# First layer's conditioning columns as float32 products in four column groups of the tensor engine, second layer's partial sums inside the first feed-forward

## The chip, the cores and the metric

The kernel is one program on one core of a Trainium2 chip. Its time is the device time of one execution in microseconds (us). The engines are named as in the profile: PE (TensorE matmuls), PEld (the weight loads that belong to them), DVE (VectorE), ACT (ScalarE), POOL (GpSimd) and SP (SyncE, which issues every DMA here).

## The reference

Two layers of a backbone block run over 512 latent tokens and 256 context tokens of width 1024. In each layer a conditioning vector gives six modulation rows per feature, one set for the latent tokens (from `c`) and one for the context tokens (from `c_ctx`):

```python
for layer in range(DEPTH):
    need_ctx = layer < DEPTH - 1
    mod = jax.nn.silu(c) @ w_ada[layer] + b_ada[layer]
    mod_c = jax.nn.silu(c_ctx) @ w_ada[layer] + b_ada[layer]
    sh1, sc1, gt1, sh2, sc2, gt2 = jnp.split(mod[:, None, :], 6, axis=-1)
    ...
    h = rmsnorm(x, g_norm1[layer]) * (1 + sc1) + sh1
    hc = rmsnorm(xc, g_norm1[layer]) * (1 + sc1c) + sh1c
    p = jnp.split(h @ w_in[layer], SPLIT_POINTS, axis=-1)
    ...
    x = x + gt1 * (jnp.concatenate([ya, yb, ym, yd], axis=-1) @ w_out[layer])
    h2 = rmsnorm(x, g_norm2[layer]) * (1 + sc2) + sh2
    x = x + gt2 * sq_relu_ffn(h2, w_ff1[layer], w_ff2[layer])
```

`w_ada[layer]` is 1024 x 6144 float32. The context tokens take the same path in the first layer; in the second, only their first norm is needed (`need_ctx` is false), so the last two thirds of that layer's columns are wanted for one vector only. The four mixers are A (windowed attention), B (dense attention), C (a chunked mLSTM) and D (a chunked state-space scan with a short convolution).

## The kernel before

Activations lie feature-major: 8 chunks of 128 features on the partitions, tokens along the free dimension (256 context, then 512 latent). Every float32 weight tile comes from HBM by an SP DMA (`wraw`, 256 KB, 4 buffers), ACT copies it to float32r (`wh`, line 176) and DVE subtracts the copy from the original (`wl`, line 177). A large product is then three float32r products, h by wh, hl by wh and h by wl, into one PSUM tile. PSUM has three kinds of tiles with two buffers each: `bulk` for the large products, `mx` and `s2` for the mixers.

The order on PE is written by the program. In each layer the mixers run A, D, C, B; each has long chains of small steps over DVE, ACT and POOL, and between these steps `fill` (class `Stream`, lines 368 to 400) emits as many of the next mixer's large products as a credit allows (tables `FILL_*`, lines 38 to 41). Then come the output projection and the feed-forward, `ffn1` (line 1302) and `ffn2` (line 1354), eight blocks each, with PE fed by large products throughout.

The conditioning columns are cut in 24 blocks of 256 columns per layer (`cb`), 1024 x 256 float32 or 1 MB each, with the 1024 rows as 8 blocks `k` of 128. `sil` holds the two vectors after SiLU, 128 x 8 x 2. Three ways of computing a block exist:

- `ada_first` (line 204), for the 8 blocks that the first norm of the first layer needs, before anything else can start. Half a block is one DMA of 512 KB (`adaw`). `ADA_FIRST` gives each half block a letter: P and V split the weights in two float32r parts as above, with the subtraction on POOL or DVE (line 229), and multiply with four columns of `silr`; D multiplies float32 weights directly with `sil2`. The stationary operand has 4 columns in all cases. The 4 x 256 result is copied by ACT (`adarow`), turned by two small products with a constant (`K_CV`), and DVE adds the bias into `mods`.
- `ada_step` (line 257) and `ada_finish` (line 246), for the other 16 blocks of the first layer and 24 of the second. A step issues 8 DMAs of 128 KB (`adar`, 2 buffers, line 270); ACT multiplies each by one entry of `sil` per partition (`adap`, 2 buffers, line 273) and POOL adds it to `acc` (line 275), per vector. This is emitted at a low priority, so that it stands behind other work of the same place. At a later step the sum over partitions is taken by PE, with `acc` stationary and a column of ones (line 252), and DVE adds the bias. For the 16 blocks of the second layer with a single vector, `acc` is first cut into three bfloat16 parts.
- Steps are called at fixed places: three in attention A (lines 697, 698 and 704), four, three and three in the streams of D, C and B (`astep`), one after attention B (line 1249), and 26 in the first layer's feed-forward (lines 1305 and 1306, 1372 and 1373). So 14 of the first layer's 16 jobs lie in its mixers, and the other 2 with all 24 of the second layer in its feed-forward.

The chain that the first norm needs is `norm_scale` (DVE, columns of 128 x 2: `sc`, `rw`, `ry`, `rc`, lines 108 to 116) and then per chunk one ACT operation, one on DVE and the subtraction `hl` on DVE or POOL (line 501).

Of the kernel before, what the change touches and what calls it, by code (L numbers as in the profile page):

```python
# [7 lines left out]
F32 = mybir.dt.float32  # L8
# [22 lines left out]
K_ID, K_LE, K_GE, K_HI, K_CV = 0, 128, 256, 384, 386  # L31
NCST = 388
# [3 lines left out]
ADA_FIRST = "PDPDPDPDPDPVDVPV"  # L36
# bulk products emitted at the steps of the mixers, by layer
# [8 lines left out]
def tile_hybrid_backbone(ctx, tc, xin, cin, wada, win0, win, wout, wf1, wf2, pcol, prow, cst, rope, out):  # L46
# [74 lines left out]
    # constants  # L121
# [23 lines left out]
    # conditioning vectors  # L145
    sil = sm((P, 8, 2), "sil")
# [4 lines left out]
    silr = sm((P, 8, 4), "silr", F32R)  # L151
    V.tensor_copy(silr[:, :, 0:2], sil)
    tt(silr[:, :, 2:4], sil, silr[:, :, 0:2].bitcast(F32), ALU.subtract)
    sil2 = sm((P, 8, 4), "sil2")
    V.memset(sil2, 0.0)
    V.tensor_copy(sil2[:, :, 0:2], sil)
# [4 lines left out]
    # weights: exact split of each float32 weight in two float32r parts; a list over the contraction's blocks  # L161
# [19 lines left out]
    # reciprocal square root of src * scale + eps on small columns  # L181
# [18 lines left out]
    # inputs, and the first norm's shift and scale on the tensor engine  # L200
    xr = [k6(r, (P, 2, NT), name="x") for r in XIN_ROLES]
    raw_roles = [0, 1, 2, 4, 5, 6, 7, 8]

    def ada_first(i, cb):
        pt_ = s2()
        o, oc = pt_[0:4, 0, 0:256], pt_[:, 1, 0:4].rearrange("p (m v) -> p m v", v=2)
        for kh in range(2):
            mode = ADA_FIRST[(2 * i + kh) % len(ADA_FIRST)]
            if i == 7:
# [3 lines left out]
                rk = [raws[k // 2][:, k % 2, :] for k in range(4)]  # L213
            else:
                raw = k6(raw_roles[(2 * i + kh) % 8], (P, 4, 256), name="adaw")
                SY.dma_start(raw, wada[0, cb, kh])
                raws = [raw]
                rk = [raw[:, k, :] for k in range(4)]
            if mode == "D":
                for k in range(4):  # L220
                    mm(o, sil2[:, 4 * kh + k, :], rk[k], kh == 0 and k == 0, kh == 1 and k == 3)
                continue
            E_ = G if mode == "P" else V
            for k in range(0, 4, 2):
                h = T((P, 2, 256), F32R, "wh", 6)
                lo = T((P, 2, 256), F32R, "wl", 6)
                w = raws[k // 2] if i == 7 else raws[0][:, k:k + 2]
                act(h, w, AF.Copy)
                E_.tensor_tensor(lo, w, h.bitcast(F32), ALU.subtract)
                for q in range(2):  # L230
                    mm(o, silr[:, 4 * kh + k + q, :], h[:, q, :], kh == 0 and k + q == 0, False)
                    mm(o, silr[:, 4 * kh + k + q, :], lo[:, q, :], False, kh == 1 and k + q == 3)
        row = tf((4, 256), name="adarow")
        act(row, o, AF.Copy)
        for m in range(2):
            mm(oc[:, m, :], row[:, m * P:(m + 1) * P], cs[0:4, K_CV:K_CV + 2])
        tt(mods[0][:, :, 2 * cb:2 * cb + 2], oc.rearrange("p m v -> p v m"),
           pcs[0][:, C_BADA + 2 * cb:C_BADA + 2 * cb + 2].unsqueeze(1).to_broadcast([P, 2, 2]), ALU.add)
# [3 lines left out]
    ada_jobs = [(0, cb, (0, 1)) for cb in range(8, 24)]  # L242
    ada_jobs += [(1, cb, (0, 1) if cb < 8 else (0,)) for cb in range(24)]
    ada_state = {"i": 0, "pend": []}

# [11 lines left out]
    def ada_step(keep=1, gate=None):  # L257
        i = ada_state["i"]
        ada_finish(keep if i < 24 else 0)
        if i >= len(ada_jobs):  # L260
            return
# [205 lines left out]
    for l in range(DEPTH):  # L467
# [827 lines left out]
        if l == 0:  # L1295
            ada_finish()
# [204 lines left out]
```

## Time and profile before

| | |
|---|---|
| times of three runs | 1895.83, 1904.86 and 1896.25 us, median 1896.25 |
| the profiled execution | span 1897.0 us |
| instructions | 31253 |
| PE busy | 1788.0 us, 94% |
| DVE busy | 1259.2 us, 66% |
| ACT busy | 991.7 us, 52% |
| POOL busy | 553.2 us, 29% |
| HBM read | 172.52 MB, 93 GB/s over the span with the writes |

The profile is of one execution, and its own time is the span, 0.75 us above the median of the three runs. Busy time is instruction time; PE and PEld overlap. The stages can be told apart in the trace by the lines that run in them: 0 to 63 us the first norm and the first conditioning blocks, 63 to 590 the first layer's mixers and output projection, 590 to 1140 its feed-forward, 1140 to 1530 the second layer's mixers, and 1530 to 1897 its feed-forward with the last norm. PEclk is the clock that the throttle granted to TensorE, as a share of full speed.

### The profile page before, as it was taken

To read this page: it belongs to the slowest core of one execution; us is meant where nothing else is said; L and a number is where in the kernel's file an instruction comes from. 1 tells how busy PE (TensorE), PEld (TensorE's weight loads), DVE (VectorE), ACT (ScalarE), POOL (GpSimd) and SP (SyncE) were. 2 spreads that over 40 slices of the span, in tenths; PEclk is the share of its full clock that TensorE was granted. 3 is DMA by queue.
4 is the path that set the end of the run, shared out by engine and by line. 5 is a ranking of instruction groups with operands and counts; after the bars stand their busy time and mean duration, and the time that the engine had idled before them with its cause. 6 is when DMAs were issued, how large, how long until landed. Compare 5 with 4: busy or idle time off the path is not lost.

```text
span 1897.0 us, 31253 instructions
## 1 busy us (share of the span) xinstructions
PE 1788.0 (94%) x11226; PEld 1566.4 (83%) x11226; DVE 1259.2 (66%) x2812; ACT 991.7 (52%) x2082; POOL 553.2 (29%) x655
## 2 busy tenths in 40 slices
PE   5989988998999999999999999999999899999998
PEld 2778887887878888888888887989877699999997
DVE  6668788478887545545645557788588765555556
ACT  4577764656666656544544536553365543333333
POOL 3354466463024655443323412005120100000000
PEclk9999999988999999999999999999999999999999
DMA  6232243223112333333333431123222023222221
GB/s 242 94 91 92 67 128 114 81 76 125 37 48 94 117 110 121 101 121 117 110 100 104 136 114 45 53 64 95 78 78 73 23 85 100 96 95 90 97 92 67
DMA packets 121146, 178.87 MB, mean 94 GB/s; under 512 B 13344, under 2 KB 62880, under 8 KB 120992
## 3 DMA queue, kind: packets, MB, share of 16 engines
q1 hardware_dynamic: 120992, 176.89, 29.3%
q8 instruction: 88, 1.44, 0.3%
q14 instruction: 66, 0.54, 0.1%
HBM read 172.52 MB, written 4.33 MB: 93 GB/s over the span
## 4 chain that ended last, share of the span: by engine, by line
PE 75%; DVE 11%; ACT 6%; POOL 3%; issue 3%; DMA 2%; SPq 0%; DVEq 0%; ACTq 0%; POOLq 0%
PE bulk L97 37%; PE s L97 28%; PE mx L97 8%; POOL acc L275 2%; PE mx L640 2%; DVE wl L108 1%; ACT qs L105 1%; ACT adap L105 1%; DMA adar<-in_wada_dram 1%; ACT wh L105 1%; DMA x<-in_xin_dram 1%; DVE rw L108 1%; ACT pr L105 0%; DVE x L116 0%; DVE xw L108 0%
## 5 line engine op out<-in xcount | busy, mean ns | idle before, releaser
L275 POOL TENSOR_TENSOR acc<-acc,adap 128x256 f32<-128x256 f32 x448 | 369.0, 842 | 393.0 <-ACT adap L105 205.1
L108 DVE TENSOR_TENSOR wl<-wraw,wh 128x512 fp32r<-128x512 f32 (+2 forms) x400 | 292.2, 735 | 117.1 <-ACT wh L105 106.7
L105 ACT ACTIVATE wh<-wraw 128x512 fp32r<-128x512 f32 (+2 forms) x404 | 243.6, 610 | 207.6 <-PE bulk L97 131.6
L105 ACT ACTIVATE adap<-adar,sil 128x256 f32<-128x256 f32 x448 | 218.0, 505 | 187.5 <-DMA adar<-in_wada_dram 127.7
L97 PE MATMUL s<-h,wh 128*128 128x258 f32 (+2 forms) x1024 | 310.6, 313 | 0.0
L97 PE MATMUL s<-hl,wh 128*128 128x258 f32 (+2 forms) x1024 | 301.0, 312 | 0.3 <-DVE hl L116 0.3
L97 PE MATMUL s<-h,wl 128*128 128x258 f32 (+2 forms) x1024 | 246.9, 312 | 0.0
L116 DVE SCALAR_TENSOR_TENSOR x<-bulk,mod,x 128x512 f32<-128x512 f32 (+1 forms) x224 | 149.5, 671 | 114.5 <-PE bulk L97 113.9
L97 PE MATMUL bulk<-ah,wh 128*128 128x512 f32 (+1 forms) x576 | 217.6, 378 | 1.4 <-DVE mod L108 0.8
L97 PE MATMUL bulk<-ah,wl 128*128 128x512 f32 (+1 forms) x576 | 215.8, 375 | 0.0
L97 PE MATMUL bulk<-al,wh 128*128 128x512 f32 (+1 forms) x576 | 215.5, 374 | 0.0
L97 PEld LDWEIGHTS s<-h,wh 128*128 128x128 f32 x1024 | 194.7, 190 | 20.9
L97 PEld LDWEIGHTS s<-hl,wh 128*128 128x128 f32 x1024 | 194.8, 190 | 12.2 <-DVE hl L116 0.7
L97 PE MATMUL bulk<-h,wh 128*128 128x512 f32 (+1 forms) x448 | 166.8, 372 | 5.1 <-DVE ra L108 3.3
L97 PEld LDWEIGHTS s<-h,wl 128*128 128x128 f32 x1024 | 163.6, 190 | 1.1
L97 PE MATMUL bulk<-hl,wh 128*128 128x512 f32 (+1 forms) x448 | 157.9, 352 | 0.0
L97 PE MATMUL bulk<-h,wl 128*128 128x512 f32 (+1 forms) x448 | 157.8, 352 | 0.0
L97 PEld LDWEIGHTS bulk<-ah,wh 128*128 128x128 f32 x576 | 108.2, 188 | 21.5 <-issue 1.2
L97 PEld LDWEIGHTS bulk<-ah,wl 128*128 128x128 f32 x576 | 108.2, 188 | 21.2
L97 PEld LDWEIGHTS bulk<-al,wh 128*128 128x128 f32 x576 | 108.2, 188 | 19.5
L105 ACT ACTIVATE relu<-relu,bs 128x512 f32<-128x512 f32 x96 | 59.0, 644 | 115.2 <-DVE relu L108 114.5
L97 PE MATMUL bulk<-wh,h 128*128 128x256 f32 (+1 forms) x368 | 113.7, 310 | 2.7 <-ACT h L105 1.6
(331 smaller groups left out, 3848.8 us busy)
## 6 DMA issues: line engine op xcount, KB each, us to landing
wraw<-in_wf_dram SPq DMA_DIRECT2D x256, 256.0 KB, 2.8
adar<-in_wada_dram SPq DMA_DIRECT2D x320, 128.0 KB, 2.4
wraw<-in_win_dram SPq DMA_DIRECT2D x80, 256.0 KB, 2.9
wraw<-in_wout_dram SPq DMA_DIRECT2D x32, 256.0 KB, 2.9
adaw<-in_wada_dram SPq DMA_DIRECT2D x14, 512.0 KB, 10.4
x<-in_xin_dram SPq DMA_DIRECT2D x8, 768.0 KB, 6.4
CB<-drows SPq DMA_DIRECT2D x10, 512.0 KB, 6.0
MB<-drows SPq DMA_DIRECT2D x10, 512.0 KB, 5.1
```

The source lines that it names most:

```text
L97: return TE.matmul(o, lhsT=l, rhs=r, start=start, stop=stop)
L105: return S.activation(o, i, f, scale=scale, **kw)
L108: return V.tensor_tensor(o, a, b, op)
L116: return V.scalar_tensor_tensor(o, a, s, b, op0, op1)
L275: G.tensor_tensor(accs[vi], accs[vi], dst, ALU.add)
L640: TE.transpose(tp[:, i, e, :], Ps[e][:, (i0 + i) * P:(i0 + i + 1) * P], ident)
```

## The change

There are three parts.

1. **The first 8 blocks.** `ada_first` no longer splits weights. `sil` lies in the first 16 columns of a tile `silw` of 48 columns, the rest zero. Row block k is a float32 product with the 32 columns of `silw` from 2k on as stationary operand; its result goes to partitions 32 x (k mod 4) on, so that the blocks k = 0 to 3 use four column groups of the array, and k = 4 to 7 add onto them. ACT copies the 128 x 256 result, PE turns it with two transposes, and one DVE reduction adds the four groups up.
2. **The first layer's other 16 blocks** use the same products (`ada0_step`): four DMAs of 256 KB (`ada`, 3 buffers) at a low priority, 8 products into a `bulk` tile, an ACT copy (`adrow`), and at the next step two transposes into another `bulk` tile, the reduction and the bias. ACT's scaling, POOL's sums and the product with ones are gone from them. All 16 now lie in the mixers: three in attention A, six in D's stream, three in C's, three in B's, one after attention B. In the streams each counts 2.0 of credit, and the totals from which the credit is worked out are raised to match (`t_ada`).
3. **The second layer's 24 blocks** keep ACT and POOL and all lie in the first layer's feed-forward. Their DMAs are 256 KB, in tiles of `ta` (5 buffers); ACT's scaling is still 256 wide, POOL's sums are 512 wide over pairs of row blocks, with one more sum of 256 at the end.

```diff
+    silw = sm((P, 48), "silw")
+    V.memset(silw, 0.0)
+    sil = silw[:, 0:16].rearrange("p (k v) -> p k v", v=2)
...
+    def ada_rows(o, kr):
+        for k, w in kr:
+            g = slice(32 * (k % 4), 32 * (k % 4) + 32)
+            mm(o[g, :], silw[:, 2 * k:2 * k + 32], w, k < 4, k >= 4)
+
+    def ada_cols(l, cb, row, oc):
+        for m in range(2):
+            TE.transpose(oc[:, m * P:(m + 1) * P], row[:, m * P:(m + 1) * P], ident)
+        r = sm((P, 2, 2), "adr", bufs=2)
+        V.tensor_reduce(r, oc.rearrange("p (m g i v) -> p v m g i", m=2, g=4, v=2)[:, :, :, :, 0], AX.X, ALU.add)
+        tt(mods[l][:, :, 2 * cb:2 * cb + 2], r,
...
-            if mode == "D":
-                for k in range(4):
-                    mm(o, sil2[:, 4 * kh + k, :], rk[k], kh == 0 and k == 0, kh == 1 and k == 3)
-                continue
-            E_ = G if mode == "P" else V
-            for k in range(0, 4, 2):
...
-                act(h, w, AF.Copy)
-                E_.tensor_tensor(lo, w, h.bitcast(F32), ALU.subtract)
...
+                ada_rows(o, [(4 * kh + k, raw[:, k, :]) for k in range(4)])
+        row = tf((P, 256), name="adarow")
         act(row, o, AF.Copy)
...
+        ada_cols(0, cb, row, oc)
...
+    def ada0_step(gate=None):
+        ada0_finish()
+        cb = ada0["i"]
...
+            raws = [T((P, 2, 256), F32, "ada", 3) for _ in range(4)]
+            for q in range(4):
+                SY.dma_start(raws[q], wada[0, cb, q // 2][:, 2 * (q % 2):2 * (q % 2) + 2, :])
+        o = bulk((P, 256))
+        ada_rows(o, [(k, raws[k // 2][:, k % 2, :]) for k in range(8)])
+        row = T((P, 256), F32, "adrow", 2)
+        act(row, o, AF.Copy)
+        ada0["pend"] = (cb, row)
...
+        with tc.high_priority(offset=-1000000):
+            acc = k4((P, nv, 2, 256), name="acc")
+            for q in range(4):
+                w = ta((P, 2, 256), name="adar")
+                SY.dma_start(w, wada[1, cb, q // 2][:, 2 * (q % 2):2 * (q % 2) + 2, :])
+                for v in range(nv):
+                    dst = acc[:, v] if q == 0 else ta((P, 2, 256), name="adap")
+                    for r in range(2):
+                        act(dst[:, r, :], w[:, r, :], AF.Copy, scale=sil[:, 2 * q + r, v:v + 1])
+                    if q > 0:
+                        G.tensor_tensor(acc[:, v], acc[:, v], dst, ALU.add)
+            for v in range(nv):
+                G.tensor_tensor(acc[:, v, 0, :], acc[:, v, 0, :], acc[:, v, 1, :], ALU.add)
...
-        astep = g_do(ada_step)
+        astep = [g_do(ada0_step, 2.0)] if l == 0 else []
+        t_ada = 2.0 * len(astep)
...
-            gs = gs[:len(od) // 2] + [gstep] + gs[len(od) // 2:] + [gstep]
-            grs.append((lambda g=g: granule(g), gs + [astep]))
+            gs = gs[:len(od) // 2] + [gstep] + (astep if i < 2 else []) + gs[len(od) // 2:] + [gstep]
+            grs.append((lambda g=g: granule(g), gs + astep))
...
-                if cb or b < 2:
-                    ada_step(0 if b == 1 and cb else 1)
+                if l == 0 and (cb or b < 2):
+                    ada_step()
```

On PE in attention A of the first layer, before the change, one job shows only as products of its sums with ones, between the attention's products with the values (`pth`, `ptl` by `VS`) and the transposes of its probabilities (`pr`).

```order
L97 MATMUL mx_1629<-ptl_1635,VS_592 128x256
L97 MATMUL bulk_1741<-ones_67,acc_955 128x1 x2
L97 MATMUL bulk_1741<-ones_67,acc_956 128x1 x2
L97 MATMUL mx_1629<-pth_1689,VS_592 128x256
L640 MATMUL mx_1709<-cst_63,pr_1504 128x128
L640 MATMUL mx_1709<-cst_63,pr_1520 128x128
```

On PE in the same attention after the change, a job is its eight products from the four tiles `ada_1494` to `ada_1497`; the two transposes of the job ahead of it stand four rows above this piece.

```order
L95 MATMUL bulk_1502<-ada_1494,silw_86 32x256 x2
L95 MATMUL bulk_1502<-ada_1495,silw_86 32x256 x2
L95 MATMUL bulk_1502<-ada_1496,silw_86 32x256 x2
L658 MATMUL mx_1513<-cst_63,pr_1301 128x128
L95 MATMUL mx_1421<-pth_1428,VS_483 128x256
L95 MATMUL mx_1421<-ptl_1427,VS_483 128x256
...
L95 MATMUL bulk_1546<-h_100,wh_1069 128x512
L95 MATMUL bulk_1546<-hl_101,wh_1069 128x512
L95 MATMUL bulk_1502<-ada_1497,silw_86 32x256 x2
```

The products of the first three tiles stand together, and those of the fourth come eight rows later: six of attention A, and two of a large product.

On SP, the queue of all DMAs, the same tiles after the change, with the weight loads (`wraw`) that stand among them:

```order
L250 DMA ada_1496<-in_wada_dram 128x512
L168 DMA wraw_1536<-in_win_dram 128x512
L168 DMA wraw_1542<-in_win_dram 128x512
L168 DMA wraw_1923<-in_win_dram 128x512
L168 DMA wraw_1929<-in_win_dram 128x512
L250 DMA ada_1497<-in_wada_dram 128x512
L250 DMA ada_1698<-in_wada_dram 128x512
```

The fourth tile of a job takes the buffer of its first, so its DMA can only be issued when the job's first two products are done.

On POOL in mixer D of the first layer, before the change, the masks of the scan (`CB`) stand among the sums of the conditioning jobs.

```order
L275 TENSOR_TENSOR acc_2627<-acc_2627,adap_2683 128x256
L275 TENSOR_TENSOR acc_2628<-acc_2628,adap_2686 128x256
L938 AFFINE_SELECT CB_3552<-CB_3552 128x512
L939 AFFINE_SELECT CB_3552<-CB_3552 128x512
L938 AFFINE_SELECT CB_3599<-CB_3599 128x512
L939 AFFINE_SELECT CB_3599<-CB_3599 128x512
```

On POOL in mixer D after the change:

```order
L924 MEMSET hst_2998 128x256
L958 AFFINE_SELECT CB_3158<-CB_3158 128x512
L959 AFFINE_SELECT CB_3158<-CB_3158 128x512
L958 AFFINE_SELECT CB_3225<-CB_3225 128x512
L959 AFFINE_SELECT CB_3225<-CB_3225 128x512
```

No conditioning sum is left on POOL ahead of the first feed-forward.

More of the change, by code (lines that the diff above doesn't have):

```diff
@@ L212, in ada_first @@
                     SY.dma_start(raws[q], wada[0, cb, kh][:, 2 * q:2 * q + 2, :])
[L213 removed]
+                ada_rows(o, [(4 * kh + k, raws[k // 2][:, k % 2, :]) for k in range(4)])
             else:
@@ L233, in ada_first @@
-        row = tf((4, 256), name="adarow")
-        act(row, o, AF.Copy)
[L235 to L244, printed above, removed]
@@ L246, in ada_finish @@
-    def ada_finish(keep=0):
-        while len(ada_state["pend"]) > keep:
-            l, cb, vs, accs = ada_state["pend"].pop(0)
-            ap_ = bulk((P, 2, 2))
-            for vi, v in enumerate(vs):
-                for m in range(2):
-                    for t, part in enumerate(accs[vi]):
-                        mm(ap_[:, vi, m:m + 1], part[:, m * P:(m + 1) * P], ones if len(accs[vi]) == 1 else onesb, t == 0, t == len(accs[vi]) - 1)
-            for vi, v in enumerate(vs):
-                tt(mods[l][:, v, 2 * cb:2 * cb + 2], ap_[:, vi, :], pcs[l][:, C_BADA + 2 * cb:C_BADA + 2 * cb + 2], ALU.add)
@@ L257, in ada_step, with ada0_finish @@
[L257 to L260, printed above, removed]
+                ada_rows(o, [(4 * kh + k, raw[:, k, :]) for k in range(4)])
+        row = tf((P, 256), name="adarow")
+        act(row, o, AF.Copy)
+        ada_cols(0, cb, row, oc)
+    ada0 = {"i": 8, "pend": None}
+    def ada0_finish():
+        if ada0["pend"] is not None:
+            cb, row = ada0["pend"]
+            ada_cols(0, cb, row, bulk((P, 256)))
+            ada0["pend"] = None
@@ L266, in ada_step @@
                 st.enter_context(tc.issue_after(gate))
-            accs = [sm((P, 256), "acc", bufs=4) for _ in vs]
-            for k in range(8):
-                w = T((P, 256), F32, "adar", 2)
-                SY.dma_start(w, wada[l, cb, k // 4][:, k % 4, :])
-                for vi, v in enumerate(vs):
-                    dst = accs[vi] if k == 0 else T((P, 256), F32, "adap", 2)
-                    act(dst, w, AF.Copy, scale=sil[:, k, v:v + 1])
-                    if k > 0:
-                        G.tensor_tensor(accs[vi], accs[vi], dst, ALU.add)
@@ new lines, in ada_finish @@
+    def ada_finish():
+        if ada_state["pend"] is None:
+            return
+        cb, parts = ada_state["pend"]
+        ada_state["pend"] = None
+        nv = len(parts)
+        ap_ = bulk((P, 2, 2))
+        for v in range(nv):
+            for m in range(2):
+                for t, part in enumerate(parts[v]):
+                    mm(ap_[:, v, m:m + 1], part[:, m * P:(m + 1) * P], ones if nv == 2 else onesb, t == 0, t == len(parts[v]) - 1)
+        for v in range(nv):
+            tt(mods[1][:, v, 2 * cb:2 * cb + 2], ap_[:, v, :], pcs[1][:, C_BADA + 2 * cb:C_BADA + 2 * cb + 2], ALU.add)
@@ L1390, in tile_hybrid_backbone @@
         ffn2(7, prev)
-        while l == 0 and ada_state["i"] < len(ada_jobs):
+        while l == 0 and ada_state["i"] < 24:
             ada_step()
```

93 lines of the change are left out of this document (43 added, 50 removed).

## Prediction

> **What bounds the kernel now.** I read the page's chain of work first, then busy time by stage, then the chain of waits inside each stage. The span, and the chain's shares by engine:
>
> ```profile
> span 1897.0 us, 31253 instructions
> PE 75%; DVE 11%; ACT 6%; POOL 3%; issue 3%; DMA 2%; SPq 0%; DVEq 0%; ACTq 0%; POOLq 0%
> ```
>
> PE holds three quarters of the chain. The busy time by stage (start:end, length, then busy time of each engine, the granted clock, DMA share):
>
> ```profile
> core 0: us, PE busy (x) PEld busy (x) DVE busy (x) ACT busy (x) POOL busy (x), PEclk, DMA share, GB/s
> 0.00:63.00 63.00, 36.80 (x180) 18.91 (x180) 44.32 (x100) 30.54 (x61) 25.38 (x27) 0.95 0.58 210
> 63.00:590.00 527.00, 485.42 (x3133) 428.34 (x3134) 405.02 (x1010) 339.16 (x775) 225.62 (x273) 0.94 0.28 85
> 590.00:1140.00 550.00, 544.07 (x3182) 475.92 (x3180) 299.12 (x543) 285.06 (x582) 225.35 (x277) 0.99 0.36 114
> 1140.00:1530.00 390.00, 364.07 (x2391) 316.27 (x2392) 304.17 (x793) 206.66 (x451) 76.86 (x79) 0.97 0.21 63
> ```
>
> The first stage (first norm) has PE busy for 37 of 63 us: DVE is ahead of it. The first layer's mixers have PE busy for 92.1% at a clock of 0.94; the second layer's, without conditioning jobs, 93.4% at 0.97. The first feed-forward is full, 544 of 550. The chains of waits by line, for the first layer's mixers, the first stage and the first feed-forward:
>
> ```profile
> by line: PE bulk L97 27.6%; PE s L97 8.2%; POOL acc L275 6.5%; issue 5.7%; PE mx L97 5.3%; PE mx L640 2.9%; ACT adap L105 2.8%; ACT qs L105 2.2%; DMA adar<-in_wada_dram 2.1%; DVE wl L108 2.0%; ACT pr L105 1.5%; DVE xw L108 1.4%; DVE CB L108
> by line: PE s L97 22.1%; DMA x<-in_xin_dram 16.7%; PE mx L97 8.4%; DVE wl L229 8.4%; issue 8.1%; DVE sq L328 6.0%; DVE x L113 5.3%; DVE rc L116 3.9%; DVE sc L116 2.7%; DVE rw L116 2.6%; DVE rw L108 2.6%; SPq L483 2.1%; DVE hl L501 1.8%; SPq
> by line: PE s L97 46.0%; PE bulk L97 36.5%; PE mx L97 15.0%; POOL acc L275 0.8%; DMA adar<-in_wada_dram 0.5%; issue 0.2%; DVE x L116 0.2%; ACT adap L105 0.2%; ACT wh L105 0.2%; DVE xn L116 0.1%; ACT xn L105 0.1%; DVE wl L108 0.1%; DVE sq L3
> ```
>
> In the mixers the conditioning job's own line runs through POOL `acc`, ACT `adap` and DMA `adar`: 6.5 + 2.8 + 2.1 = 11.4% of 527, or 60 us. In the feed-forward it is 0.8 + 0.5 + 0.2 = 1.5% of 550, 8 us. So the change attacks the mixers and the first stage.
>
> **First stage.** Its POOL and DVE subtractions, then three DVE operations on two columns each:
>
> ```profile
> L229 POOL TENSOR_TENSOR wl<-adaw,wh 128x512 fp32r<-128x512 f32 x12 | 16.0, 1352 | 27.4 <-ACT wh L105 27.4
> L229 DVE TENSOR_TENSOR wl<-adaw,wh 128x512 fp32r<-128x512 f32 x4 | 3.1, 797 | 0.0
> L229 DVE TENSOR_TENSOR wl<-wraw,wh 128x512 fp32r<-128x512 f32 x2 | 2.4, 1197 | 0.0
> 35.02 2.53 POOL L229 TENSOR_TENSOR wl<-adaw,wh 128x512 fp32r<-128x512 f32 x2 [1.27 <-ACT wh L105]
> 36.25 1.31 DVE L116 SCALAR_TENSOR_TENSOR sc<-mod,pcol 128x2 f32<-128x2 f32 x2
> 37.67 0.16 DVE L116 SCALAR_TENSOR_TENSOR ry<-rw,ry 128x2 f32<-128x2 f32 x1
> ```
>
> Two columns take DVE 0.16 us, but two such operations took 1.31 us while POOL subtracted. The six subtractions on DVE go, and the chain gives them 8.4% of 63 us = 5.3 us. The held columns `rc`, `sc` and `rw` have 3.9 + 2.7 + 2.6 + 2.6 = 11.8% = 7.4 us; most of that, which I put at 5.7, goes with POOL's 16 us. Added are 8 reductions of a few columns, 8 x 0.16 = 1.3 us at most, mostly in waits for `adaw`. I take -11 us, from -5 (DVE's own subtractions alone) to -13 (all of both). PE, with 26 us idle, hides its 16 transposes.
>
> **First layer's mixers, what goes.** The groups of the job in this stage, and for scale the transposes of A and B:
>
> ```profile
> L275 POOL TENSOR_TENSOR acc<-acc,adap 128x256 f32<-128x256 f32 x203 | 165.7, 840 | 237.9 <-ACT acc L105 130.5 <-ACT adap L105 104.0 <-PE mx L640 2.8
> L105 ACT ACTIVATE adap<-adar,sil 128x256 f32<-128x256 f32 x203 | 97.9, 505 | 62.1 <-POOL acc L275 31.1 <-DMA adar<-in_wada_dram 25.4 <-POOL MB L1166 4.8
> L97 PE MATMUL bulk<-ones,acc 128*128 128x1 f32 x112 | 15.6, 259 | 1.2 <-POOL acc L275 1.2
> L640 PE MATMUL mx<-cst,pr 128*128 128x128 f32 x200 | 33.2, 283 | 5.8 <-ACT pr L105 4.1 <-DVE ptl L108 1.2 <-DVE yB L108 0.3
> ```
>
> POOL loses 166 us, ACT about 100, PE 15.6 us of products with ones (14 jobs). ACT waits 31 us for POOL inside the job, and whatever of the mixers is queued behind such a wait on ACT is late with it. DVE gains too, since its operations last longer beside POOL's: the same operation in the first layer's mixers and in the second's,
>
> ```profile
> L108 DVE TENSOR_TENSOR es<-prow,m 128x1 f32<-128x1 f32 x24 | 7.5, 311 | 0.0
> L108 DVE TENSOR_TENSOR es<-prow,m 128x1 f32<-128x1 f32 x16 | 2.4, 152 | 0.0
> ```
>
> The upper end of this relief is the chain's 60 us. The lower end is PE's busy time at the second layer's share: 485.4 / 0.934 = 520, 7 us less. With that stage's clock as well it is 485.4 x 0.94 / 0.97 / 0.934 = 504, 23 us less. I take -34, the middle of 7 and 60: a chain's 60 us is not all won, because other chains lie just under it, but the job's work is gone from three engines and not from one.
>
> **First layer's mixers, what PE gains in work.** The float32 products of the first stage, a pair of 64-column groups (`vw`) among large products, DVE's eviction of a large product, and the landing time of DMAs of 256 KB and, when the queue is crowded, of 512 KB:
>
> ```profile
> 32.12 1.89 PE L97 MATMUL s<-adaw,sil 128*4 128x256 f32 x8
> L97 PEld LDWEIGHTS s<-adaw,sil 128*4 128x4 f32 x48 | 3.9, 95 | 8.1 <-issue 4.5 <-DVE mod L108 0.8
> 349.85 0.28 PE L97 MATMUL bulk<-wl,h 128*128 128x256 f32 x1
> 349.97 0.28 PE L97 MATMUL bulk<-wh,hl 128*128 128x256 f32 x1
> 350.18 0.45 PE L97 MATMUL mx<-vw,ktok 128*64 128x65 f32 x8
> 350.56 0.39 PE L97 MATMUL bulk<-wh,h 128*128 128x256 f32 x1
> L116 DVE SCALAR_TENSOR_TENSOR x<-bulk,mod,x 128x512 f32<-128x512 f32 (+1 forms) x224 | 149.5, 671 | 114.5 <-PE bulk L97 113.9
> wraw<-in_win_dram SPq DMA_DIRECT2D x80, 256.0 KB, 2.9
> adaw<-in_wada_dram SPq DMA_DIRECT2D x14, 512.0 KB, 10.4
> ```
>
> The 8 records in 1.89 us are 4 products: two records each, one after another, about 0.213 us apiece (the last one's tail taken off). A job has 8 products, 16 records: 16 x 0.213 = 3.41 us if column groups take turns. The row of `vw` says that they do not: 8 records of 65 columns in two groups take 0.45 us with one tail of about 0.22, 33 ns a record, where 0.213 x 65 / 256 = 54 ns would be the serial rate. Four groups at once and the order of the products (0 to 3, 4 and 5, later 6 and 7) make three rounds of two records: 6 x 0.213 = 1.28 us; if only two groups overlap, 1.7. Going into the groups and out costs more than the 0.12 us step between large products: 0.21 before `vw`, and after it about as much, so 0.2 us an excursion; two excursions, 0.4. Two transposes, at 33.2 / 200 = 0.166 each, 0.33. Together 2.0 us (two groups: 2.4; switching free and transposes at half: 1.5). For 16 jobs 32 us (38; 24), less the 15.6: **+16 us**, from +8 to +23. This is not hidden: PE is the bound.
>
> The Trainium skill ("TensorE: Matmul & The Clock Gate", Part 3, The mechanism) speaks against this: it lets a weight load overlap running products only when the row group differs, and four column groups share all rows. If it held here, the 95 ns load of each record would be exposed, 16 x 16 x 0.095 = 24 us, an estimate from this rule and the row; by it the sum below ends at 1898. The trace disagrees as far as it goes, since 33 ns a record leaves no room for 95 ns loads in the open.
>
> **Waits that it adds.** The fourth tile of a job needs the buffer of the first, so its DMA starts only after the job's first two products, and PE, which runs in order, stands at products 6 and 7 until it lands, with all large products and mixer steps behind. A landing takes 2.9 us, with 0.2 allowed for release and issue 3.1. What stands between, by the order and dense rows (0.12 us for 256 columns, 0.24 for 512), is 0.9 to 5.9 us, mean 2.9. In the piece shown it is 0.43 + 0.43 + 0.14 + 5 x 0.12 + 2 x 0.24 = 2.1 us, so a wait of 1.0. Over the 16 jobs the missing parts add to 9 us; at a landing of 4, 5 or 6 us to 21, 35 or 50. The job also holds one of two `bulk` buffers meanwhile, so a large product in the other one may wait for its eviction: 16 x 0.67 = 11 us at most, 2 taken, because mixer products fill most of these gaps. **+11 us**, from +2 to +20. On SP the weight loads behind a blocked `ada` DMA are needed 20 us or more after it is freed by the same count, which covers the few us; without that cover each would cost its landing.
>
> **First feed-forward.** It has two jobs fewer, and POOL's sums are fewer and wider; their 8 us on the chain may go: **-4 us**, from 0 to -8. The second layer's 24 jobs were there before, ACT's part of each is unchanged, and a finished sum is wanted some 100 PE products later, so nothing new waits. The second layer's modulations are all ready before its first norm.
>
> **Sum** against the profiled 1897.0: -11 - 34 + 16 + 11 - 4 = -22, 1875.0; the median of the runs shown lies 0.75 lower, so **1874 us**. About 0.5%, or 9.5 us, is what a measurement of this kernel can tell from no change.
>
> **Rivals.**
> - *The whole chain share is won* (60 in place of 34): 1848. For it: the jobs' 11.4% of the chain, and a clock that could rise. Against: PE is 92% busy there already.
> - *The mixers are held by something else* (7 in place of 34): 1901, no change. For it: DVE is busy for 405 of 527 us, 77%, and in the second layer's mixers for 304 of 390, 78%, without any job; PE's share there is only 1.3 points higher. Against: the clock, and DVE's shorter operations.
> - *Column groups run one after another*: 3.41 in place of 1.28 us a job, +34: 1908. Against it: `vw`.
> - *Slower: PE stands at the fourth tile in every job.* If a landing takes 6 us where several transfers queue, waits are 50 and not 9: +41, 1915. It decides from waits of about 41 us on, a landing of some 5.4 us. For it: SP issues the fourth tile with the next job's tiles and weight loads, and `adaw` took 10.4 us in the crowded first stage. Against: the mixers move 85 GB/s, where 256 KB land in 2.9 us.
>
> **How the numbers follow.** Forecast 0.50 (its own range 1858 to 1890, from relief and added work going half-way to their ends), whole share 0.15, held by something else 0.14, serial 0.05, slower 0.16. Faster by over 0.5% (below 1887): 0.46 of the forecast and the 0.15, 0.61. Within: 0.04 + 0.13 + 0.01 = 0.18. Slower (above 1906): 0.16 + 0.04 + 0.01 = 0.21. The range runs from 1842, under the whole share, to 1908, which leaves out most of the slower case.
>
> **What would show it.** First stage: first large product near 52 us instead of 63. Mixers: `ada` products with records 50 to 60 ns apart in a round and about 2 us of PE per job; waits of PE for DMA `ada` near 9 us; `es` near 0.15 us; the stage 7 us shorter (34 less 27) at a clock of 0.96 or more. Feed-forward: about 546 us. Wrong if the records of a job stand 0.21 us apart, if waits for `ada` pass 40 us, or if the mixers' stage is longer than 527.

## The result, and the profile after

The changed kernel took 1908.86 us (median of 9 runs, 1906.49 to 1914.86), the kernel before 1896.25 us (9 runs). The ratio is 1.0069, interval 1.0053 to 1.0086: slower by 0.7%, where 1.2% faster was forecast, and just outside the range. The profiled execution after was the slowest of its nine (1914.86 us, 6 us above the median), the one before lay some 2.5 us above its median, so differences of stages hold about 3.5 us more than the medians do. The chain of work after, by engine:

```profile
span 1913.1 us, 30450 instructions
PE 77%; DVE 8%; ACT 5%; DMA 4%; issue 3%; POOL 2%; SPq 0%; DVEq 0%; ACTq 0%; POOLq 0%
```

DVE, ACT and POOL have a smaller share of the chain, as intended, and PE and DMA a larger one. To see where the time went, the stages are cut at the same events in both traces: first large product, first product of the feed-forward, first large product of the second layer, first product of its feed-forward. These are not the prediction's stages: its cut at 590 us lies 38 us behind the first product of the feed-forward (551.6 us). The columns are those of the prediction's table: start:end, length, then busy time of PE, PEld, DVE, ACT and POOL (with the number of instructions), the granted clock, DMA share and GB/s. Busy time by stage before the change:

```profile
0.00:63.04 63.04, 36.84 (x181) 18.93 (x181) 44.36 (x100) 30.58 (x61) 25.42 (x27) 0.95 0.58 210
63.04:551.60 488.56, 448.38 (x2920) 396.43 (x2920) 374.36 (x934) 312.99 (x720) 212.96 (x258) 0.93 0.28 87
551.60:1141.40 589.80, 581.12 (x3395) 507.85 (x3393) 331.14 (x620) 312.56 (x639) 237.99 (x293) 0.99 0.35 110
1141.40:1505.80 364.40, 341.54 (x2216) 295.10 (x2217) 282.97 (x736) 191.39 (x414) 67.86 (x68) 0.97 0.21 65
1505.80:1897.00 391.20, 380.13 (x2522) 348.06 (x2520) 226.37 (x426) 144.22 (x252) 8.98 (x11) 0.99 0.27 88
```

and after it:

```profile
0.00:49.76 49.76, 25.55 (x168) 12.06 (x168) 31.58 (x99) 20.43 (x40) 6.39 (x12) 0.96 0.72 263
49.76:546.10 496.34, 459.22 (x3102) 383.67 (x3102) 343.64 (x941) 229.07 (x518) 61.38 (x70) 0.95 0.29 91
546.10:1146.40 600.30, 583.63 (x3368) 507.80 (x3366) 346.23 (x613) 282.83 (x600) 193.50 (x160) 0.98 0.32 104
1146.40:1520.90 374.50, 347.70 (x2216) 300.51 (x2217) 281.68 (x736) 191.95 (x414) 65.03 (x68) 0.95 0.20 63
1520.90:1913.00 392.10, 380.77 (x2522) 348.62 (x2520) 226.61 (x426) 144.67 (x252) 9.04 (x12) 0.99 0.27 88
```

| stage | before | after | difference | forecast |
|---|---|---|---|---|
| first norm | 63.0 | 49.8 | -13.3 | -11 |
| first layer's mixers | 488.6 | 496.3 | +7.8 | -7 |
| first feed-forward | 589.8 | 600.3 | +10.5 | -4 |
| second layer's mixers | 364.4 | 374.5 | +10.1 | 0 |
| second feed-forward | 391.2 | 392.1 | +0.9 | 0 |

The first stage did what was said, and a little more. The mixers lost where they should have won, and 20 us went in two places that the forecast held for safe: the first feed-forward, and the second layer's mixers, in which the program is almost the same. Single profiles of a stage scatter, though. The runs below hold more profiles of the first layer's mixers: four in the form of before, 483.2 to 488.8 us, and three in the changed form, 489.3 to 494.0. So the mixers lost about 6 us in the mean, and less or more in a single pair. Four of PE's waits after the change (waiting line, what it waits for, us in total, times, longest) show where to look:

```profile
PE s L95 <- DMA adaw<-in_wada_dram: 17.1, 1, 17.1
PE bulk L95 <- POOL acc L294: 10.2, 7, 3.7
PE bulk L95 <- DMA ada<-in_wada_dram: 8.1, 7, 2.1
...
PE mx L916 <- DVE yA L106: 5.3, 1, 5.3
```

The first row is only the load of the first columns at the start. The second lies in the feed-forward, the third in the first layer's mixers (7 of the 16 jobs waited, each time for the fourth tile), the last in the second layer's mixers.

The new products themselves, in one job of mixer work at 164 us (start, duration, number of records):

```profile
164.31 0.38 PE L658 MATMUL mx<-cst,pr 128*128 128x128 f32 x2
164.62 1.06 PE L95 MATMUL bulk<-ada,silw 128*32 128x256 f32 x12
165.61 0.39 PE L95 MATMUL bulk<-h,wh 128*128 128x256 f32 x1
...
167.73 0.28 PE L95 MATMUL bulk<-h,wl 128*128 128x256 f32 x1
167.94 0.63 PE L95 MATMUL bulk<-ada,silw 128*32 128x256 f32 x4
168.50 0.33 PE L658 MATMUL mx<-cst,pr 128*128 128x128 f32 x1
```

Twelve records take 1.06 us with the last one's tail. One after another they would take 12 x 0.213 = 2.6 us, so the column groups do run at once. One by one, the eight records of products 0 to 3 start in two sets of four, 7 ns apart within a set, and the four of products 4 and 5, which use two of the groups, in two sets of two; the sets follow at 0.22 to 0.24 us. The last four records (products 6 and 7) stand in a burst of their own, that is, behind other products, and each burst pays for going in and out: 0.21 us ahead of the second, where 0.12 is the step of large products, and 0.56 from its first record to the product behind it.

### The profile page after: what moved, and what is told of

Its sections match the earlier page's. It is cut to its first block, busy times and chain, and to the rows that moved or that the text cites. A ratio compares the mean times of both kernels' runs of the same rounds, so it can differ in the third digit from the quotient of the medians.

```text
span 1913.1 us, 30450 instructions
## 1 busy us (share of the span) xinstructions
PE 1796.9 (94%) x11370; PEld 1552.7 (81%) x11370; DVE 1229.7 (64%) x2811; ACT 869.0 (45%) x1822; POOL 335.3 (18%) x321
## 4 chain that ended last, share of the span: by engine, by line
PE 77%; DVE 8%; ACT 5%; DMA 4%; issue 3%; POOL 2%; SPq 0%; DVEq 0%; ACTq 0%; POOLq 0%
PE bulk L95 40%; PE s L95 26%; PE mx L95 8%; PE mx L658 2%; DMA CB<-drows 1%; DMA ada<-in_wada_dram 1%; DMA adar<-in_wada_dram 1%; POOL acc L292 1%; ACT wh L103 1%; DVE wl L106 1%; ACT qs L103 1%; DMA adaw<-in_wada_dram 1%; DMA wraw<-in_wout_dram 1%; ACT adap L103 1%; DVE x L114 0%
## 5 line engine op out<-in xcount | busy, mean ns | idle before, releaser
L106 DVE TENSOR_TENSOR wl<-wraw,wh 128x512 fp32r<-128x512 f32 (+2 forms) x400 | 282.5, 712 | 114.0 <-ACT wh L103 105.1
L292 POOL TENSOR_TENSOR acc<-acc,adap 128x512 f32<-128x512 f32 x96 | 141.3, 1479 | 413.3 <-ACT acc L103 220.7
L95 PEld LDWEIGHTS bulk<-al,wh 128*128 128x128 f32 x576 | 108.8, 189 | 19.5
L95 PE MATMUL bulk<-wl,h 128*128 128x256 f32 (+1 forms) x368 | 110.0, 300 | 2.0 <-DVE wl L106 1.9
## 6 DMA issues: line engine op xcount, KB each, us to landing
adaw<-in_wada_dram SPq DMA_DIRECT2D x14, 512.0 KB, 10.5
```

The costliest lines, as they stand in the source:

```text
L95: return TE.matmul(o, lhsT=l, rhs=r, start=start, stop=stop)
L106: return V.tensor_tensor(o, a, b, op)
L292: G.tensor_tensor(acc[:, v], acc[:, v], dst, ALU.add)
```

## The experiments

Each edit below is shown in part where it is long; `...` marks what is left out. Behind a time stand its lowest and highest run, then the ratio to runs of the kernel before taken beside it, with its 95% interval.

Theory after the comparison: the change has three separate losses, each with its own cause. In the first feed-forward the sums over partitions are taken at the very next step, before POOL is done. In the second layer the work stands in another order on DVE and PE. In the mixers the jobs cost PE more, and relieve less, than forecast. Rivals were that the jobs had become too slow, that the second layer's loss was the clock by chance, and that the mixers are held by something else.

**One step's delay for the sums.** The kernel before takes a job's sum two steps after its loads for the jobs with two vectors (but for one step); the changed one at the next step. This edit restores the delay in the changed kernel (`pend` becomes a list).

```diff
     def ada_step():
-        ada_finish()
+        ada_finish(1 if ada_state["i"] < 8 else 0)
...
-        ada_state["pend"] = (cb, parts)
+        ada_state["pend"].append((cb, parts))
```

> The changed kernel, with the sums over partitions of the second layer's first eight jobs taken one step later, as the kernel before did. Theory: the first feed-forward lost its 10.5 us (589.8 to 600.3) because PE now reaches the ones-products of a job just when POOL ends it (waits for POOL acc 10.2 us in 7 times); with a step in between these waits fall below 3 us and the stage comes back to about 590. With this edit the order of the second layer on PE and DVE is also that of before, so if the order is what cost it 10 us, its mixers (first large product to first feed-forward product) come back from 374.5 to about 364.4. Together about 20 us less than the changed kernel: 1889. Rival 1: the jobs themselves have become too slow (wider sums, transfers of 256 KB), so a step's delay only moves the wait: stage near 600. Rival 2: the second layer lost its time to the granted clock and not to its order: mixers stay near 374, and the kernel comes to about 1899.

1891.34 us (1888.69 to 1896.03, 11 runs), 0.998, 0.9969 to 0.9991: 17.5 us less than the changed kernel. In the changed kernel a piece of the feed-forward shows the mechanism, PE first, then POOL:

```profile
638.53 0.39 PE L95 MATMUL s<-hl,wh 128*128 128x512 f32 x1
640.13 0.61 PE L95 MATMUL bulk<-ones,acc 128*128 128x1 f32 x4 [1.21 <-POOL acc L294]
```

```profile
637.60 1.29 POOL L292 TENSOR_TENSOR acc<-acc,adap 128x512 f32<-128x512 f32 x1 [2.44 <-ACT adap L103]
638.97 1.11 POOL L294 TENSOR_TENSOR acc<-acc 128x256 f32<-128x256 f32 x1
```

POOL's last sum ends at 640.08, and PE's product with ones starts at 640.13: PE was there first and stood. With the delay the wait row becomes

```profile
PE bulk L95 <- POOL acc L294: 2.3, 2, 1.3
```

and the stage 580.8 us in place of 600.3:

```profile
543.40:1124.20 580.80, 573.60 (x3368) 501.64 (x3367) 348.38 (x613) 281.87 (x600) 194.34 (x160) 1.00 0.34 108
```

This is 19.5 us for 8 us of waits for `acc`. PE's idle time in the stage (length less busy time) fell from 16.7 to 7.2 us, which is 9.5. Most of the rest is the granted clock, 0.98 over the stage with the waits and 1.00 without. In the changed kernel it was 0.50 in three stretches among these waits, which the kernel with the delay does not have:

```profile
598.70:602.10 3.40, 3.40 (x18) 3.40 (x17) 1.65 (x5) 2.43 (x5) 0.00 (x0) 0.50 0.23 77
619.20:626.00 6.80, 6.05 (x21) 4.95 (x20) 3.06 (x9) 1.87 (x4) 1.18 (x2) 0.50 0.25 80
660.20:667.00 6.80, 6.80 (x19) 5.12 (x18) 0.98 (x3) 0.43 (x2) 2.24 (x3) 0.50 0.14 41
```

Half of their 17 us is 8.5, so idle time and clock make 18 of the 19.5 us. The waits need not be long for it: ahead of the first stretch stand two, of 0.61 and 0.47 us. The stage is now 9 us shorter than before the change. Rival 1 is out. The second half of the expectation failed: the second mixers stayed at 374.1, with `PE mx L916 <- DVE yA` at 5.1 us. The statement that their order would be that of before was wrong: in this kernel they stand in the changed kernel's order.

**Empty steps in the second layer's streams.** In the kernel before, `astep` is called in the second layer too, does nothing there and takes 0.05 of credit; in the changed kernel the steps are gone.

```diff
-        astep = [g_do(ada0_step, 2.0)] if l == 0 else []
-        t_ada = 2.0 * len(astep)
+        astep = [g_do(ada0_step, 2.0)] if l == 0 else [g_do(lambda: None)]
+        t_ada = 2.0 if l == 0 else 0.0
...
-            gs = gs[:len(od) // 2] + [gstep] + (astep if i < 2 else []) + gs[len(od) // 2:] + [gstep]
+            gs = gs[:len(od) // 2] + [gstep] + (astep if l == 0 and i < 2 else []) + gs[len(od) // 2:] + [gstep]
```

> The changed kernel, with empty steps put back into the second layer's streams (0.05 of credit each), which gives its order on PE and DVE as before. Theory: the second layer's mixers took 10 us more only because DVE and PE have their work in another order there (PE waits 5.3 us for yA at the start of mixer D): 374.5 becomes about 364.4 and the kernel about 1899; the first feed-forward stays at 600. Rival: the clock was lower by chance or by what went before, and the mixers stay near 374, the kernel near 1909.

1903.55 us (1897.62 to 1907.57, 12 runs), 1.0038, 1.0026 to 1.0051: 5.3 us less than the changed kernel. The wait for `yA` is gone, the second mixers took 370.0 us, not the 364.4 that was expected, and the feed-forward kept its waits for POOL (10.1 us, stage 599.6). The other order is seen on DVE. Before, the last piece of `yA` stands ahead of the mask subtractions of mixer D (`CB`), and in the changed kernel behind two of them:

```profile
1284.45 0.29 DVE L108 TENSOR_TENSOR yA<-mx,tm 128x128 f32<-128x128 f32 x1
...
1285.26 1.22 DVE L108 TENSOR_TENSOR CB<-CB,cum 128x1024 f32<-128x1024 f32 x1
```

```profile
1285.27 1.23 DVE L106 TENSOR_TENSOR CB<-CB,cum 128x1024 f32<-128x1024 f32 x1 [1.46 <-POOL CB L959]
...
1290.03 1.68 DVE L106 TENSOR_TENSOR CB<-CB,cum 128x1024 f32<-128x1024 f32 x1
...
1295.96 0.29 DVE L106 TENSOR_TENSOR yA<-mx,tm 128x128 f32<-128x128 f32 x1
```

What the wait costs is seen in the changed kernel's trace, before, right behind, and some us behind it (busy times, then the clock):

```profile
1285.00:1290.90 5.90, 5.90 (x33) 4.98 (x31) 5.63 (x6) 3.41 (x6) 5.28 (x7) 1.00 0.44 149
1296.40:1301.70 5.30, 5.30 (x25) 5.30 (x26) 4.18 (x9) 1.29 (x3) 0.00 (x0) 0.50 0.62 201
1301.90:1310.00 8.10, 8.10 (x72) 8.10 (x71) 6.55 (x12) 4.41 (x9) 2.32 (x2) 1.00 0.00 0
```

```profile
1296.40 0.66 PE L916 MATMUL mx<-cst,fD 128*128 128x128 f32 x2 [5.25 <-DVE yA L106]
1296.71 0.56 PE L95 MATMUL bulk<-wh,h 128*128 128x256 f32 x1
1297.07 0.41 PE L95 MATMUL bulk<-wl,h 128*128 128x256 f32 x1
1297.28 0.41 PE L95 MATMUL bulk<-wh,hl 128*128 128x256 f32 x1
```

After 5.25 us of waiting the clock is 0.50 for 5.3 us, and the products at 1297 us are 0.21 us apart, where 0.12 is the undisturbed step. So the wait costs about 5.25 + 2.6 = 8 us. The Trainium skill ("TensorE: Matmul & The Clock Gate", Part 1, What's actually happening) says this: after an idle window of about 3.4 us PE runs at half rate until it has been busy for such a window. This place agrees: the granted clock reads 0.50 from 1295.1 to 1301.9 us, 6.8 us, of which 1.3 lie in the wait. The first stretch in the feed-forward above does not need an idle window of that length: in the 3.4 us ahead of it PE was busy for 2.31.

**Both losses put into the kernel before.** To test the two causes from the other side, each was added alone to the kernel before: the sums of the second layer's two-vector jobs without the delay, and the second layer's streams without the empty steps.

```diff
-        ada_finish(keep if i < 24 else 0)
+        ada_finish(keep if i < 16 else 0)
```

> The kernel before, with one thing of the change: the sums over partitions of the second layer's first eight jobs are taken at the very next step and not one step later. Theory: this alone makes PE wait for POOL's sums in the first feed-forward, as in the changed kernel: the stage grows by about 10 us, from 589.8 to 600, with waits of PE for POOL acc near 10 us in place of 2.6, and the kernel comes to about 1906. Rival: the smaller transfers and sums of before end their jobs in time, so that nothing is waited for: 1896.

1904.15 us (1901.16 to 1912.3, 11 runs), 1.0039, 1.0024 to 1.0055: slower by 8 us. In the profile, of a run of 1912.3 us, the stage took 599.4 us in place of 589.8. The loss is near what was expected, the waits are not: PE waited in this stage for `acc` 4.7 us in place of 2.6, where 10 were expected. All its idle time there rose from 8.7 to 13.2 us, and the granted clock read 0.98 in place of 0.99, some 6 us. So the missing delay costs this kernel time as well, but less of it in open waits.

```diff
-        astep = g_do(ada_step)
+        astep = [g_do(ada_step)] if l == 0 else []
...
-                [g_tok(j, hs, 280, ev_z(j)) for j in first_tok] + [gstep, astep])]
+                [g_tok(j, hs, 280, ev_z(j)) for j in first_tok] + [gstep] + astep)]
...
```

> The kernel before, without the empty steps in the second layer's streams, so that its order on DVE there is that of the changed kernel. Theory: PE waits some 5 us for yA at the start of the second layer's mixer D, and the kernel takes about 5 us more, 1901; its second mixers go from 364 to 370 or more. Rival: the order costs nothing by itself, and the stage was slower for another reason: 1896.

1905.51 us (1901.15 to 1908.05, 8 runs), 1.0051, 1.003 to 1.0071: slower by 9.3 us, more than expected. The second mixers took 375.0 us, and the wait is there:

```profile
PE mx L896 <- DVE yA L108: 4.9, 1, 4.9
```

Over all 13 kernels of this document, the five without the empty steps have this wait, of 4.8 to 5.4 us, and the eight with them do not. The second mixers took 372.2 to 375.0 us in the five profiles and 364.4 to 370.3 in the eight; the means are 5.8 us apart. The kernel before, with 364.4 at a granted clock of 0.97, is the lowest of the eight: the kernel of "The first stage alone" below, with the same program in this stage, has 368.4 at 0.95. So about 6 of the +10.1 us are the order, and the rest is scatter between executions, of the clock by these two rows.

**The mixers without their jobs.** The changed kernel without the first layer's 16 jobs: the columns 2048 to 6143 of its conditioning are neither loaded nor multiplied. The steps keep their credit in the streams.

```diff
     def ada0_step(gate=None):
-        ada0_finish()
         cb = ada0["i"]
         if cb >= 24:
             return
+        V.tensor_copy(mods[0][:, :, 2 * cb:2 * cb + 2], ...)
+        ada0["i"] = cb + 1
+        return
```

> The changed kernel without the 16 jobs of the first layer's mixers: no weights are loaded and multiplied for the columns 2048 to 6143 of that layer, whose modulations are the bias alone. This shows what the mixers take with no conditioning work at all (before 488.6 us, changed 496.3, from the first large product to the first of the feed-forward). Theory: the relief from ACT and POOL was about 19 us and not 34, so that the stage without any job is 488.6 less 19 less 15.6 of products with ones, about 454, and the jobs on PE cost 496.3 less 454, some 42 us: 32 of products, 8 of waits for their tiles. Rival 1 (the relief was 34 as forecast): 439, and the jobs cost 57. Rival 2 (the mixers are held by something else, relief 7): 466, and the jobs cost 30.

1857.01 us (1853.82 to 1862.95, 4 runs). The mixers' stage:

```profile
47.10:493.60 446.50, 417.86 (x2812) 370.21 (x2811) 336.54 (x907) 222.41 (x501) 63.15 (x70) 0.96 0.21 63
```

Without any job it is 446.5 us. The 14 jobs on ACT and POOL had cost it 488.6 - 446.5 = 42 us, and on PE the 16 jobs cost 496.3 - 446.5 = 50, about 3 us a job both times; with the other profiles of these two forms it is 37 to 42 and 43 to 50. Less the 15.6 us of products with ones, the relief was 26.5 us (21 to 27): between the theory (19) and the forecast (34), and not the 7 of something else holding the mixers. Part of the 42 is the clock, 0.93 over this stage before and 0.96 here: some 34 us lost to it in the one and 18 in the other, an estimate from these rows.

**All products in one column group**, to price the groups.

```diff
-            g = slice(32 * (k % 4), 32 * (k % 4) + 32)
-            mm(o[g, :], silw[:, 2 * k:2 * k + 32], w, k < 4, k >= 4)
+            mm(o[0:32, :], silw[:, 2 * k:2 * k + 32], w, k == 0, k == 7)
...
```

> The changed kernel with all eight products of a block in one column group, one after another onto the same 32 partitions (the two transposes take 32 rows). Theory: the four groups ran at once, so a job's 16 records now take 16 x 0.213 = 3.4 us in place of about 1.3, and the first layer's mixers, where PE is the bound, grow by 16 x 2.1 = 34 us, from 496 to about 530; the kernel comes to some 1943. Rival: part of the products lay in time in which PE waited anyway, so that the stage grows by half of it or less, to 513.

1941.77 us in one run, with 1943 expected. The groups of the products in the layer's jobs, changed kernel and then this one (busy, mean ns):

```profile
L95 PE MATMUL bulk<-ada,silw 128*32 128x256 f32 x256 | 32.4, 434 | 11.0 <-DMA ada<-in_wada_dram 8.1 <-DVE x L114 0.9 <-DVE kcq L1035 0.6
```

```profile
L95 PE MATMUL bulk<-ada,silw 128*32 128x256 f32 x256 | 67.6, 411 | 4.3 <-DMA ada<-in_wada_dram 2.6 <-DVE kcq L1034 0.6 <-DVE ra L106 0.4
```

The same 256 records keep PE busy for 67.6 us in place of 32.4. The mixers grew by 23 us (519.4), not 34, and the waits for the fourth tile fell from 8.1 to 2.6 us, being covered by longer products; the first norm grew by 5.4 us (55.2). So the whole came out near the expected time in part by luck: the first norm made up for half of what the mixers lacked, and the changed kernel's profile, with which the stages are compared, lies 6 us above its median. The groups pay, and the rival that they run in turn is out.

**Both repairs together.**

> The changed kernel with both repairs: the sums of the second layer's first eight jobs one step later, and the empty steps in the second layer's streams. Theory: the two add, since they act on different stages: the first feed-forward at about 581 as with the first repair alone, the second layer's mixers at about 369 as with the second: 1891.3 less 5, 1886. Rival: the second repair's 5 us was the clock of its runs, and the kernel stays at 1891.

1884.96 us (1877.43 to 1895.83, 12 runs), 0.9948, 0.993 to 0.9967. The two add: first feed-forward 580.3, second mixers 367.2. With both repairs the kernel is 11 us faster than before, half of the 22 that were forecast.

**The fourth tile in a weight buffer**, on top of both repairs.

```diff
-            raws = [T((P, 2, 256), F32, "ada", 3) for _ in range(4)]
+            raws = [T((P, 2, 256), F32, "ada", 3) for _ in range(3)] + [T((P, 2, 256), F32, "wraw", 4)]
```

> As the kernel with both repairs, and the fourth tile of each of the first layer's 16 jobs in a weight buffer (wraw) and not in the buffer of the job's first tile, so that its transfer does not wait for the job's own products. Theory: the waits of PE for ada, 8 to 10 us, go, and with them the pauses that they bring: mixers from 494 to about 485, the kernel about 9 us under the one with both repairs, 1877. Rival: the weight loads, which now share their four buffers with these tiles, come late, and PE waits for wl or wh in place of ada: no gain, 1886 or more.

1867.42 us (1860.55 to 1875.56, 6 runs), 0.9843, 0.9818 to 0.9868. This beats both kernels, and it gave twice what was expected: the mixers went from 489.3 to 471.1, in profiles of runs of 1877.43 and 1860.55 us. A job is now one burst (two of the 16 are still split):

```profile
158.79 0.27 PE L658 MATMUL mx<-cst,pr 128*128 128x128 f32 x1
158.99 0.84 PE L95 MATMUL bulk<-ada,silw 128*32 128x256 f32 x10
159.46 0.39 PE L95 MATMUL bulk<-wraw,silw 128*32 128x256 f32 x2
159.66 0.39 PE L95 MATMUL bulk<-ada,silw 128*32 128x256 f32 x2
159.68 0.39 PE L95 MATMUL bulk<-wraw,silw 128*32 128x256 f32 x2
159.99 0.39 PE L95 MATMUL bulk<-h,wh 128*128 128x256 f32 x1
```

All 16 records lie between 158.99 and 159.68, four sets of four, and the large product behind them starts at 159.99: 1.0 us. The changed kernel needed 165.61 - 164.62 = 0.99 us for twelve, as long as sixteen take here, and 168.50 - 167.94 = 0.56 for the other four. Products 6 and 7 fill up the sets of two that 4 and 5 leave, so in one burst they cost nothing. The waits for `ada` are gone, and so is one entry and exit in each job. Added up over the jobs, from the record ahead of a burst to the record behind it, PE spent 54.8 us on them in the kernel with both repairs (34 bursts) and 33.1 here (19 bursts). That is 21.7 us, of which 8.4 were waits for the tiles. A second burst without a wait takes, by the rows of the changed kernel, 0.21 + 0.56 us in place of a step of 0.12: over 16 jobs 10 us, an estimate. The other 3 us were not measured apart.

**A second job later in attention A**, on top of that: the second job is called after two of the four query products, in place of right behind the first.

```diff
             ada0_step(gate=last_dma[0])
-            ada0_step()
...
+            if l == 0 and n_ == 2:
+                ada0_step()
```

> As the kernel with both repairs and the fourth tile in a weight buffer, with the second of the first layer's jobs called between the second and third large product of attention A's queries and not right behind the first job. Theory: the first two jobs stand back to back, so that PE waits 3 us for the copy adrow and about as long for the second job's tiles; with large products between them these waits go, and the kernel comes to about 1862 in place of 1867. Rival: the waits move to the third job, and nothing is gained: 1867.

1865.6 us (1863.53 to 1870.24, 5 runs), 0.9837, 0.9815 to 0.986: not told apart from 1867.42. The 3.0 us wait for `adrow` is still there, now of a large product for the `bulk` buffer that the copy reads.

**The first stage alone**, in the kernel before (`ada_rows`, `ada_cols`, `ada_first` and `silw` of the change, all else as before).

> The kernel before, with only the first eight blocks computed as in the changed kernel. Theory: the first large product starts at about 50 us in place of 63.0, and the 13 us stay won to the end, since what follows is unchanged: about 1883. Rival: the earlier start is given back in the mixers, because the conditioning jobs there and the clock set their pace: about 1893 or no change.

1880.77 us (1879.11 to 1889.63, 6 runs), 0.9928, 0.9908 to 0.9947. The first large product starts at 50.6 us, and the gain stays to the end. This part alone is as good as the whole change with both repairs (0.9948): until the fourth tile was moved, the other parts had won nothing beside it.

**First stage changed, the other jobs of the first layer as before, the second layer's as changed with the delay** (a step runs the old code until the 16 jobs are done, then the new).

> The first eight blocks as changed, the first layer's other 16 as before (ACT and POOL, 14 of them in the mixers), and the second layer's 24 in the changed form with the sums of the first eight one step later. Theory: the jobs cost the mixers 42 us on ACT and POOL and 50 on PE, so this keeps the mixers near 488.7; with the first stage at 50 and a feed-forward of about 583, it comes some 5 us under the kernel that changes the first stage alone (1880.8): 1876. Rival: the feed-forward gained in the run with the later sums because it had two jobs fewer, and with them it stays at 588: 1881.

1889.78 us (1883.92 to 1892.55, 11 runs), 0.9956, 0.9941 to 0.997. Neither expectation came out: the feed-forward took 597.4 us, 16.6 more than with the later sums above. This edit takes the last first-layer sums without a delay, and PE waits for them, once for 7.6 us in the feed-forward:

```profile
PE bulk L97 <- POOL acc L265: 8.8, 3, 7.6
```

With the clock there at 0.99 in place of 1.00, some 6 us, this is most of the 16.6. So the run points again at a missing delay and does not answer what it was made for: whether two jobs fewer made the feed-forward shorter stays open.

## Why the prediction was wrong

*First stage: right.* -13.3 against -11. The mechanism is seen in the operations on two columns, before and after, which POOL's subtractions no longer hold up:

```profile
L116 DVE SCALAR_TENSOR_TENSOR sc<-mod,pcol 128x2 f32<-128x2 f32 x6 | 2.8, 510 | 0.0
```

```profile
L114 DVE SCALAR_TENSOR_TENSOR sc<-mod,pcol 128x2 f32<-128x2 f32 x8 | 0.9, 155 | 0.1
```

*Relief of the mixers: right in kind, too large.* 26.5 us (21 to 27) against 34, near the estimate from the second layer's share and clock (23). The middle between 7 and 60 leaned too much on the chain's 60 us. DVE did become quicker, as forecast:

```profile
L106 DVE TENSOR_TENSOR es<-prow,m 128x1 f32<-128x1 f32 x24 | 3.6, 154 | 0.1
```

*PE's work and waits in the mixers: right, or a little too small.* The forecast gave the jobs 32 + 11 = 43 us, and they cost 43 to 50. The overlap of four groups and the waits for the fourth tile (8.1 us against 9) were right. The rule of the Trainium skill that was weighed ("TensorE: Matmul & The Clock Gate", Part 3, The mechanism), on weight loads that only overlap where the row group differs, does not hold here: 16 records in 1.0 us leave no room for 16 loads of 116 ns, their mean in this kernel. The kernel with the fourth tile in a weight buffer shows that the waits for that tile and the split of a job cost about 18 us together, where their terms in the sum were 9 us of waits and 0.2 us for the second excursion of each job, 3 us. Still, the mixers' stage grew where 7 us less were forecast, mostly for the relief; a longer stage was one of the prediction's own signs of being wrong.

*First feed-forward: the step that failed.* "A finished sum is wanted some 100 PE products later, so nothing new waits" was read from the order, in which PE's product with ones does stand far behind the loads, and the price of -4 us rested on it. But POOL ends a job's sum only about one step after its loads (at 640.08 us in the piece above, with PE already there), and the delay of one step that `keep` gave the two-vector jobs was the cover. The change removed it. Cost: +10.5 in place of -4, shown by restoring it (the stage at 580.8, which is -9) and by taking it out of the kernel before (+8 us). So the saving was there, more than forecast, and the waits with the slow clock behind them took 19.5 us from it.

*Second layer's mixers: a term that was not in the sum.* The forecast gave nothing for it, since no job runs there. Taking out empty steps changed the order on DVE and PE, and PE then stands 5.25 us for `yA`. Shown from both sides: -5.3 us when they are put back, +9.3 us when they are taken out of the kernel before. By the profiles the order is worth about 6 us, and the rest of the +10.1 is scatter.

The base was misread as well, without harm: a run's time is its span and about 1.8 us more (1891.9 beside a span of 1890.1 us), so the profiled execution of before lay some 2.5 us above the median and not 0.75. The median less 22 is 1874 either way. The slower rival named the place of a real wait, the fourth tile, but not what made the kernel slower: these waits stayed at 8 us, where it needed 41. The rival of column groups in turn gave 1908, almost the measured time, by chance alone: the groups did run at once, and putting them in turn took 33 us more. What turned a gain into a loss were the two stages outside the argument, 24 us by the medians (1908.86 against 1884.96).

Open are the 3 us that the one-burst kernel won beyond the waits and the split; the granted clock reads 0.97 over the mixers of both kernels. Open is also why the feed-forward became 9 us shorter with the delay in place, since two jobs fewer, wider sums and fewer transfers were not tried apart.

## What to carry to other kernels

When work moves between engines, list every lag and every empty step that the diff removes, and ask for each whose completion it covered: a sum taken one step earlier cost 8 to 18 us here, where the whole first stage won 13. Give PE a job whole: the same products in two bursts, with a transfer that waits for the first burst, cost 18 us over 16 jobs. And price PE's waits with the half-clock stretch that can follow them, here half as much again for one wait of 5.25 us, and about as much again for many of 0.5 to 3.7 us.

## What the runs showed of the hardware

Four float32 products with 32 stationary columns each run at once in four column groups: records start in sets of four, 7 ns apart, one set each 0.22 to 0.24 us, and 16 records take 1.0 us from the first to the next large product. Twelve of them, of which the last four use two groups only, take 0.99 us. A wait of 5.25 us was followed by 5.3 us at a granted clock of 0.50, and in the first feed-forward stretches of 3.4 and 6.8 us at 0.50 stand among waits of 0.5 to 3.7 us. An operation of DVE on two columns took 155 ns in the mean without POOL's subtractions in that stage and 510 with them.
